# Early mod columns, sums behind splits, projection weights a step ahead, and grouped matmuls in a diffusion backbone

## The chip, the cores and the metric

The kernel runs on one core of a Trainium2 chip, with its engines TensorE (PE), VectorE (DVE), ScalarE (ACT), GpSimd (POOL) and SyncE (SP, which here issues all transfers). The metric is the device time of one execution in microseconds, as the median over runs. Lower is better.

## The reference, cut to what matters

Two layers over 256 latent tokens of width 2048, with 256 context tokens in the first layer. Layer 0 mixes by latent attention (8 heads, low-rank queries, keys and values) and by a multi-scale pooling, layer 1 by a Fourier transform; each layer ends with a squared-ReLU MLP of width 8192. Shifts, scales and gates come from a modulation of the condition `c`.

```
mod = silu(c) @ w_mod[l] + b_mod[l]              # 6 vectors of 2048 per layer
sh1, sc1, g1, sh2, sc2, g2 = split(mod, 6)
hx = rmsnorm(x, norm1[l]) * (1 + sc1) + sh1
# layer 0: px = hx @ w_in, pc = hc @ w_in (hc from the context, in the same way)
#   q  = rmsnorm(px[:512]) @ w_uq        kv = rmsnorm(p[512:768]) @ w_ukv
#   attention over 512 keys, 8 heads; pool = (window means - u) @ w_pool, u = px[832:]
#   y  = concat(attention, pool) @ w_out
# layer 1: y = real(fft2(hx in 4 channel groups)) @ w_out
x = x + g1 * y
x = x + g2 * square(relu((rmsnorm(x, norm2[l]) * (1 + sc2) + sh2) @ w1[l])) @ w2[l]
```

## The kernel before

Everything is held transposed, features on the 128 partitions and tokens along the columns. Weights arrive in float32, by 1 MB tiles into a ring of six buffers W (`load`, line 121). A tile is used as a sum of two rounded parts: `split` (line 131) has ScalarE cast a piece to H (line 135) and VectorE subtract, L = W − H (line 136), into two rings of six buffers. Activations are split likewise and hold both parts side by side, 256 columns each. One product of a weight block with the tokens is then, in `wide` (line 147), a 512-column matmul of H with both parts and a 256-column matmul of L with the high part, one after the other for each of two 128-row blocks k and each of four output banks j. `narrow` does the same in three 256-column matmuls.

The modulation vectors of which `mod_vector` makes a list are computed off TensorE: `mod_step` (line 93) loads 128 columns of `w_mod` into a W buffer, and `mod_sums` (line 99) has VectorE multiply it with the broadcast `cb` = silu(c) and sum it, one instruction of 2048 elements per column ("sum" below, line 103). `load` makes all sums outstanding before each weight transfer, and issues further columns at a rate `pace`.

The order of SP and TensorE is that of the program; the order of VectorE and ScalarE is set by a scheduler at build time, and each engine then works through its list in order.

The work goes in stages, by the trace: 0 to 152 us the modulation of layer 0 and the latents (`latents`, banks ka for keys, qa for queries, pu for the pooling's inputs), 152 to 399 attention woven with pooling and output projection (`weave`), 413 to 1104 the MLP of layer 0, 1104 to 1254 the Fourier layer and its output projection w_oo, 1266 to 1988 the MLP of layer 1.

The generator `attention` first computes squares, the variances (var), their reciprocal roots, spread over partitions (rb, copied to rk and rq), the normalised key latents kvf with their parts kvh and kvl, the query latents ql with parts qls, and the rotary key kr. `project(pr)` then loads the up-projections w_ukv and w_uq of two heads and multiplies: kn (keys), qr and qn (queries), v (values). `scores` (sc), `turned` (transposes tr) and `values` (pv) follow for each head. The generator `pooling` supplies the matmuls in between: four tiles w_pl[1, kt] (banks pu, line 467), each in two halves, then the window means with four tables `band`, w_pool, and the output projection w_oe.

Of the kernel before, what the change touches and what calls it, by code (L numbers as in the profile page):

```python
# [16 lines left out]
P = 128  # L17
T = 256
D = 2048
NB = D // P  # L20
# [23 lines left out]
def hybrid_dit(ctx: ExitStack, tc: tile.TileContext, xT, ctxT, c2, cb_in, vecs, wmod_s, wmod0, wmod1,  # L44
# [32 lines left out]
    def half(b, i):  # L77
        return b[:, i * T:(i + 1) * T]

    def mm(o, l, r, start, stop):  # L80
        nc.tensor.matmul(o, l, r, start=start, stop=stop, skip_group_check=True)  # L81


    todo, late = [], []
    pace = [0.0, 0.0]
    whole = set()

    def mod_vector(l, which, norm=None):
        src = wmod0[which - 2] if l == 0 else wmod1[which]
        for j in range(NB):  # L90
            todo.append((l, which, norm, j, src[j]))

    def mod_step():
        l, which, norm, j, src = todo.pop(0)
        w = wp.tile([P, 2048], F32, name="W", tag="W")
        nc.sync.dma_start(w, src)
        late.append((w, l, which, norm, j))

    def mod_sums():

        while late:
            w, l, which, norm, j = late.pop(0)
            nc.vector.scalar_tensor_tensor(w, w, 1.0, cb, ALU.mult, ALU.mult,  # L103
                                           accum_out=mods[l][:, which, j:j + 1])
            if j == NB - 1:
                whole.add((l, which))
                v = mods[l][:, which]
                b = V_BM[l] + which * NB
                nc.vector.tensor_tensor(v, v, vec[:, b:b + NB], ALU.add)
                if norm is not None:  # L110
                    scales(mods[l], which, norm)
# [7 lines left out]


    def load(src, n=2048):
        mod_sums()
        w = wp.tile([P, 2048], F32, name="W", tag="W")
        nc.sync.dma_start(w[:, :n], src)
        pace[1] += pace[0]
        while pace[1] >= 1 and todo:
            pace[1] -= 1
            mod_step()
        return w

    def split(w, lo, n, nn):

        h = hp.tile([P, 1024], F32R, name="H", tag="H")
        l = hp.tile([P, 1024], F32R, name="L", tag="L")
        nc.scalar.copy(h[:, :n], w[:, lo:lo + n])  # L135
        nc.vector.tensor_tensor(l[:, :n], w[:, lo:lo + n], h.bitcast(F32)[:, :n], ALU.subtract)  # L136
        return [(h[:, i:i + nn], l[:, i:i + nn]) for i in range(0, n, nn)]

    def split_act(u, src, n=T):
# [3 lines left out]
    def split_pair(h, l, src):  # L143
        nc.scalar.copy(h, src)
        nc.vector.tensor_tensor(l, src, h.bitcast(F32), ALU.subtract)

    def wide(ps, wts, j, acts, first, last):

        js = slice(j * P, (j + 1) * P)
        n = len(wts)  # L150
        for k, (h, l) in enumerate(wts):
            mm(ps, h[:, js], acts[k], first and k == 0, False)
            mm(ps[:, T:], l[:, js], acts[k][:, :T], False, last and k == n - 1)

    def narrow(o, wts, j, acts, first, last):

# [14 lines left out]
    def linear(tiles, acts, evac, nb=4, slim=False, drain=False):  # L171


        if slim:
            banks = [bank() for _ in range(nb // 2)]
            ps = [half(banks[j // 2], j % 2) for j in range(nb)]
        else:
            ps = [bank() for _ in range(nb)]
        for i, (srcs, k0) in enumerate(tiles):
            for s, src in enumerate(srcs):  # L180
                w = load(src)
                final = i == len(tiles) - 1
                for k in (0, 2):
                    wts = split(w, k * 512, 1024, 512)
                    first, last = i == 0 and k == 0, final and k == 2
                    part = acts[k0 + k:k0 + k + 2]
                    if drain and final:
                        if k == 0:
                            held = wts
                            yield  # L190
                            continue
                        wts, part = held + wts, acts[k0:k0 + 4]
                    for j in range(4):
                        o = ps[4 * s + j]
                        if slim:
                            narrow(o, wts, j, part, first and j % 2 == 0, last and j % 2 == 1)
                        else:
                            wide(o, wts, j, part, first, last)

                        if last and not slim:  # L200
                            evac(4 * s + j, o)
                        elif last and j % 2:
                            evac(4 * s + j - 1, ps[4 * s + j - 1])
                            evac(4 * s + j, o)
                    yield

    def run(steps):
        for _ in steps:
            pass
# [213 lines left out]
        lat = latents(g, wkq, wpl)  # L423
    nc.sync.dma_start(cb, cb_in)
    nc.scalar.activation(cb, cb, AF.Silu)
    run(lat)

    ropet = funit("ropet")
    nc.sync.dma_start(ropet.rearrange("p (a b) -> p a b", b=T), rope)
    bandt = [funit(f"band{i}") for i in range(4)]  # L430
    for i in range(4):
        nc.sync.dma_start(bandt[i], band[:, i])

    mod_vector(0, 2)
    mod_vector(0, 4, V_N2[0])
    mod_vector(0, 3)
    pace[0] = 1.75


# [27 lines left out]
    def pooling():  # L467

        ut = [[funit("ut") for hf in range(2)] for tb in range(2)]
        for tb in range(2):  # L470
            nc.scalar.copy(ut[tb][0], pu0[tb])
        us = [bank(f"pu{tb}") for tb in range(2)]
        for kt in range(4):
            w = load(w_pl[1, kt])
            for i in range(2):
                for n, (h, l) in enumerate(split(w, 1024 * i, 1024, 512)):
                    by_token(us, 4 * kt + 2 * i + n, h, l)
                yield
        for tb in range(2):
            nc.scalar.copy(ut[tb][1], us[tb])  # L480
        yield
        pooled = []
        for g in range(4):
            ps = bank("pl")
            for j in range(2):
                fs = slice((g % 2) * T + j * P, (g % 2) * T + (j + 1) * P)
                for tb in range(2):
                    mm(half(ps, j), ut[tb][g // 2][:, fs], half(bandt[g], tb), j == 0 and tb == 0, j == 1 and tb == 1)
            pooled.append(funit("pl"))
            nc.scalar.copy(pooled[g], ps)  # L490
            if g % 2:
                yield
        w = load(w_pool)
        for g in range(4):
            ps = bank("po")
            for j in range(2):
                plain(half(ps, j), [w[:, k * 256:(k + 1) * 256] for k in (2 * g, 2 * g + 1)], j,
                      [half(pooled[g], 0), half(pooled[g], 1)], j == 0, j == 1)
            for j in range(2):
                u = unit("mx")  # L500
                sc, o = column(V_PS + 2 * g + j), half(ps, j)
                nc.scalar.mul(u[:, :T], o, sc)
                nc.vector.scalar_tensor_tensor(u[:, T:], o, sc, u.bitcast(F32)[:, :T], ALU.mult, ALU.subtract)
                mixed.append(u)
            if g % 2:
                yield
        for ng in range(4):
            yield from linear([((w_oe[ng, kt],), 4 * kt - 8) for kt in (2, 3)], mixed,
                              residual(0, 2, None, True)(ng), 4, True)
# [4 lines left out]
    def rotary(s):  # L514
# [4 lines left out]
        nc.vector.tensor_tensor(r, r, half(ropet, 1), ALU.mult)  # L519
        nc.vector.tensor_tensor(s, s, r, ALU.add)  # L520

    def attention():
        squares = []
        for b in ka[:2] + qa:
            squares.append(funit("lq"))
# [26 lines left out]
            split_act(ql[j], f)  # L552
        kr = funit("kr")
        nc.scalar.copy(kr, ka[2])
        rotary(half(kr, 1))
        krh, krl = unit("krh"), unit("krl")
        split_pair(krh, krl, kr)
        yield 2

        def project(pr):  # L560

            w = load(w_ukv[pr], 1024)
            wkv = split(w, 0, 1024, 512)
            kn, vt = [], []
            for j in range(2):
                js = slice(j * P, (j + 1) * P)
# [5 lines left out]
                    mm(ps, l[:, js], kvh[k], False, k == 1)  # L572
                kn.append((unit("knh"), unit("knl")))
                split_pair(*kn[j], ps)
            w = load(w_uq[pr], 1536)
            wuq = split(w, 0, 768, 384) + split(w, 768, 768, 384)
            ps = bank("qr")
            narrow(half(ps, 0), wuq, 2, ql, True, True)
            f = scr("qr")
# [67 lines left out]
            split_act(a, o)  # L647
            attn.append(a)

        pair = project(0)  # L650
        yield 1
        p = scores((pair, 0))
        yield 2
        for h in range(NH):
            us = turned(p)
            head = (pair, h % 2)
            if h < NH - 1:
                if h % 2:
                    pair = project(h // 2 + 1)
                    yield 1  # L660
                p = scores((pair, (h + 1) % 2))
            else:
                yield 1
            values(head, us)
            yield 2
# [257 lines left out]
```

## Time and profile before

| what | value |
|---|---|
| median of 3 runs | 2003.67 us (2002.9 to 2005.29) |
| profiled execution | 2004.05 us |
| its span | 2002.3 us |
| TensorE busy | 1937.5 us, 97% |
| VectorE busy | 1461.3 us, 73% |
| ScalarE busy | 1025.0 us, 51% |
| read from memory | 533.69 MB, 268 GB/s over the span |

The busy time of an engine counts instructions that overlap only once. Matmuls are pipelined: each begins before the one ahead of it has ended, so the time that one costs is the distance between starts, not its duration.

### The profile page before, as it was taken

The numbers are of one execution on the slowest core, as the hardware profiler recorded it, in microseconds if no ns is written. First come the engines' busy times: TensorE is split into PE (matmuls) and PEld (weight loads), VectorE is DVE, ScalarE is ACT, GpSimd is POOL, SyncE is SP. The second block draws the span as 40 slices with busy tenths as digits, with TensorE's granted clock in tenths as the row PEclk, the third lists the DMA queues.
The fourth block names the chain that finished last, engine by engine and source line by source line (L and its number), as shares of the span: only waits on it lengthen the run. The fifth ranks groups of instructions, "written<-read, shape, count | busy, mean of one in ns | idle before, by whom it ended". The sixth has DMA issues, their size and how long they took to land.

```text
span 2002.3 us, 29622 instructions
## 1 busy us (share of the span) xinstructions
PE 1937.5 (97%) x11848; PEld 1702.7 (85%) x11848; DVE 1461.3 (73%) x2042; ACT 1025.0 (51%) x1655; POOL 1.2 (0%) x13
## 2 busy tenths in 40 slices
PE   5997999989999999999999999999999999999997
PEld 3886889978888888888888989788888888888887
DVE  4447999999888888888888577897555555555564
ACT  4334554455545645554555454555455446545653
POOL 0000000000000000000000000000000000000000
PEclk8998999989999999999999999899999999999998
DMA  9996899969889889888988247597555555555541
GB/s 377 370 385 235 324 365 336 340 237 388 320 336 344 338 311 345 323 326 315 335 326 316 85 171 271 186 386 289 178 193 184 184 186 189 190 189 182 182 163 43
DMA packets 77466, 537.71 MB, mean 269 GB/s; under 512 B 8848, under 2 KB 9104, under 8 KB 14480
## 3 DMA queue, kind: packets, MB, share of 16 engines
q1 hardware_dynamic: 77328, 535.82, 72.0%
q8 instruction: 92, 1.51, 0.3%
q14 instruction: 46, 0.38, 0.1%
HBM read 533.69 MB, written 2.10 MB: 268 GB/s over the span
## 4 chain that ended last, share of the span: by engine, by line
PE 92%; DVE 6%; DMA 1%; issue 1%; ACT 1%; SPq 0%; DVEq 0%; ACTq 0%
PE mm L81 80%; PE ka L81 2%; DVE W L103 2%; PE pu L81 2%; PE mrow L81 1%; DVE L L136 1%; PE qa L81 1%; PE f L81 1%; PE sc L81 1%; PE pv L81 1%; DMA W<-in_wmod_s 0%; PE var L81 0%; PE p L81 0%; PE pl L81 0%; DMA x<-in_xT 0%
## 5 line engine op out<-in xcount | busy, mean ns | idle before, releaser
L136 DVE TENSOR_TENSOR L<-W,H 128x1024 fp32r<-128x1024 f32 (+1 forms) x620 | 744.1, 1214 | 353.6 <-ACT H L135 353.0
L135 ACT CAST H<-W 128x1024 fp32r<-128x1024 f32 (+1 forms) x620 | 640.5, 1044 | 547.0 <-PE mm L81 498.1
L81 PE MATMUL mm<-h,H 128*128 128x512 f32 x2048 | 722.3, 397 | 3.6 <-DVE h L266 3.6
L81 PE MATMUL mm<-hid,H 128*128 128x512 f32 (+1 forms) x2176 | 718.4, 382 | 0.0
L81 PE MATMUL mm<-h,L 128*128 128x256 f32 x2048 | 576.6, 282 | 0.0
L81 PE MATMUL mm<-hid,L 128*128 128x256 f32 x2048 | 574.6, 281 | 0.0
L81 PEld LDWEIGHTS mm<-hid,H 128*128 128x128 f32 x2176 | 399.8, 188 | 84.5
L81 PEld LDWEIGHTS mm<-h,H 128*128 128x128 f32 x2048 | 386.5, 189 | 95.0 <-issue 2.1
L81 PEld LDWEIGHTS mm<-h,L 128*128 128x128 f32 x2048 | 389.5, 190 | 0.0
L81 PEld LDWEIGHTS mm<-hid,L 128*128 128x128 f32 x2048 | 387.4, 189 | 0.0
L103 DVE SCALAR_TENSOR_TENSOR W<-W,cb 128x2048 f32<-128x2048 f32 x160 | 364.7, 2282 | 0.0
L454 DVE SCALAR_TENSOR_TENSOR x<-mm,mods,x 128x256 f32<-128x256 f32 x176 | 80.2, 478 | 47.3 <-ACT rt L453 24.1
L453 ACT ACTIVATE rt<-mm,mods 128x256 f32<-128x256 f32 x132 | 61.8, 469 | 57.8 <-PE mm L81 56.1
L81 PE MATMUL mm<-fr,H 128*128 128x512 f32 (+1 forms) x320 | 91.0, 352 | 0.0
L692 ACT ACTIVATE rl<-g 128x256 f32<-128x256 f32 x128 | 53.2, 415 | 60.7 <-DVE g L690 59.4
L81 PE MATMUL mm<-fr,L 128*128 128x256 f32 x256 | 72.3, 282 | 1.5 <-DVE L L136 1.5
L689 ACT COPY b<-mm 128x256 f32<-128x256 f32 x128 | 45.6, 357 | 52.6 <-PE mm L81 52.6
L81 PEld LDWEIGHTS mm<-fr,H 128*128 128x128 f32 x320 | 55.8, 188 | 8.9
L690 DVE TENSOR_TENSOR g<-mm,b 128x256 f32<-128x256 f32 x128 | 53.4, 417 | 13.7 <-ACT b L689 13.6
L693 ACT ACTIVATE hd<-rl 128x256 f32<-128x256 f32 x128 | 53.2, 415 | 2.2
L141 DVE TENSOR_TENSOR hid<-hd,hid 128x256 fp32r<-128x256 f32 x128 | 53.5, 418 | 0.4
L140 ACT CAST hid<-hd 128x256 fp32r<-128x256 f32 x128 | 52.1, 407 | 1.0
(219 smaller groups left out, 1570.8 us busy)
## 6 DMA issues: line engine op xcount, KB each, us to landing
W<-in_w SPq DMA_DIRECT2D x256, 1024.0 KB, 5.0
W<-in_wmod SPq DMA_DIRECT2D x160, 1024.0 KB, 6.5
W<-in_wmod_s SPq DMA_DIRECT2D x32, 1024.0 KB, 9.6
W<-in_w_oe SPq DMA_DIRECT2D x16, 1024.0 KB, 7.3
W<-in_w_oo SPq DMA_DIRECT2D x16, 1024.0 KB, 4.9
W<-in_w_pl SPq DMA_DIRECT2D x8, 1024.0 KB, 7.0
W<-in_w_kq SPq DMA_DIRECT2D x8, 896.0 KB, 5.9
W<-in_w_uq SPq DMA_DIRECT2D x4, 768.0 KB, 4.5
```

The lines of the kernel that those rows point to most:

```text
L81: nc.tensor.matmul(o, l, r, start=start, stop=stop, skip_group_check=True)
L103: nc.vector.scalar_tensor_tensor(w, w, 1.0, cb, ALU.mult, ALU.mult, accum_out=mods[l][:, which, j:j + 1])
L135: nc.scalar.copy(h[:, :n], w[:, lo:lo + n])
L136: nc.vector.tensor_tensor(l[:, :n], w[:, lo:lo + n], h.bitcast(F32)[:, :n], ALU.subtract)
L140: nc.scalar.copy(u[:, :n], src)
L141: nc.vector.tensor_tensor(u[:, n:2 * n], src, u.bitcast(F32)[:, :n], ALU.subtract)
L453: nc.scalar.mul(t, half(ps, 1), g)
L454: nc.vector.scalar_tensor_tensor(x[:, i], ps[:, :T], g, x[:, i], ALU.mult, ALU.add)
L689: nc.scalar.copy(b, half(ps, 1))
L690: nc.vector.tensor_tensor(s, half(ps, 0), b, ALU.add)
L692: nc.scalar.activation(r, s, AF.Relu)
L693: nc.scalar.square(f, r)
```

## The change

- `cb` is now followed at once by the transfers of two modulation columns, ahead of the last step of the latents, and their sums are made right after it.
- `load` now makes only sums of columns that are at least two loads old; each `split` makes one sum of a column at least one load old, behind its own L.
- The four band tables, loaded in one block before, are loaded one at a time, after each tile of the pooling.
- The up-projections of a pair of heads are loaded and split by `pair_weights`: for pair 0 at the start of `attention`, for the others at the start of every odd head, ahead of its transposes. The rotation of kr comes after the first `project`.
- `linear` calls `wides` where it called `wide`: for a half-step of two k and four j, all eight H matmuls, and then all eight L matmuls. The evacuations follow in the second half.

VectorE, where the pooling starts. W with cb is a sum, h the last activation of the latents, va the first instruction after the variances. Before:

```order
L266 SCALAR_TENSOR_TENSOR h<-xr,mods_102,h 128x256
L136 TENSOR_TENSOR L<-W,H 128x1024 x2
L103 SCALAR_TENSOR_TENSOR W,mods_102<-W,cb 128x2048
L237 TENSOR_SCALAR va<-var 128x4
L237 TENSOR_SCALAR va<-var 128x2
```

After:

```order
L105 SCALAR_TENSOR_TENSOR W,mods_102<-W,cb 128x2048
L288 SCALAR_TENSOR_TENSOR h<-xr,mods_102,h 128x256
L105 SCALAR_TENSOR_TENSOR W,mods_102<-W,cb 128x2048
L139 TENSOR_TENSOR L<-W,H 128x1024
L105 SCALAR_TENSOR_TENSOR W,mods_102<-W,cb 128x2048
L139 TENSOR_TENSOR L<-W,H 128x768 x2
L105 SCALAR_TENSOR_TENSOR W,mods_102<-W,cb 128x2048 x2
L139 TENSOR_TENSOR L<-W,H 128x1024 x2
L105 SCALAR_TENSOR_TENSOR W,mods_102<-W,cb 128x2048
L259 TENSOR_SCALAR va<-var 128x4
```

The two L of 1024 columns before are those of the first pooling tile; after, they are the last such row, behind five sums and the L of w_ukv (1024) and w_uq (768 twice).

VectorE a little later, from the normalised latents to the second pooling tile. Before:

```order
L136 TENSOR_TENSOR L<-W,H 128x1024
L543 SCALAR_TENSOR_TENSOR kvf<-ka_113,vec,rk 128x512
L136 TENSOR_TENSOR L<-W,H 128x1024
L145 TENSOR_TENSOR kvl<-kvf,kvh 128x512
L543 SCALAR_TENSOR_TENSOR kvf<-ka_114,vec,rk 128x512
L549 SCALAR_TENSOR_TENSOR ql<-qa_111,vec,rq 128x256 x2
L145 TENSOR_TENSOR kvl<-kvf,kvh 128x512
L549 SCALAR_TENSOR_TENSOR ql<-qa_112,vec,rq 128x256 x2
L141 TENSOR_TENSOR qls<-ql,qls 128x256 x4
```

After:

```order
L574 SCALAR_TENSOR_TENSOR kvf<-ka_113,vec,rk 128x512
L580 SCALAR_TENSOR_TENSOR ql<-qa_111,vec,rq 128x256 x2
L150 TENSOR_TENSOR kvl<-kvf,kvh 128x512
L574 SCALAR_TENSOR_TENSOR kvf<-ka_114,vec,rk 128x512
L580 SCALAR_TENSOR_TENSOR ql<-qa_112,vec,rq 128x256 x2
L150 TENSOR_TENSOR kvl<-kvf,kvh 128x512
L146 TENSOR_TENSOR qls<-ql,qls 128x256 x4
L139 TENSOR_TENSOR L<-W,H 128x1024 x2
L105 SCALAR_TENSOR_TENSOR W,mods_102<-W,cb 128x2048 x2
L150 TENSOR_TENSOR knl<-kn,knh 128x512 x2
```

The two L of the second pooling tile stood ahead of and between the kvf, and now stand behind the last qls.

SP at the first pooling loads. Before:

```order
L429 DMA ropet<-in_rope 128x512
L432 DMA band_1499<-in_band 128x512
L432 DMA band_1500<-in_band 128x512
L432 DMA band_1501<-in_band 128x512
L432 DMA band_1502<-in_band 128x512
L124 DMA W<-in_w_pl 128x2048
L96 DMA W<-in_wmod 128x2048
L124 DMA W<-in_w_pl 128x2048
L96 DMA W<-in_wmod 128x2048 x2
L124 DMA W<-in_w_ukv 128x1024
```

After:

```order
L97 DMA W<-in_wmod 128x2048 x2
L457 DMA ropet<-in_rope 128x512
L127 DMA W<-in_w_ukv 128x1024
L97 DMA W<-in_wmod 128x2048
L127 DMA W<-in_w_uq 128x1536
L97 DMA W<-in_wmod 128x2048 x2
L127 DMA W<-in_w_pl 128x2048
L97 DMA W<-in_wmod 128x2048 x2
L502 DMA band_1505<-in_band 128x512
L127 DMA W<-in_w_pl 128x2048
L97 DMA W<-in_wmod 128x2048 x2
L502 DMA band_1506<-in_band 128x512
```

The first pooling tile comes behind five columns and the two up-projections, and from the second on a band stands ahead of each tile.

The diff, without the comments and the places that only follow from it:

```diff
+    loads = [0]
     def mod_step():
-        late.append((w, l, which, norm, j))
+        late.append((loads[0], w, l, which, norm, j))
-    def mod_sums():
-        while late:
-            w, l, which, norm, j = late.pop(0)
+    def mod_sums(n=NB, old=0):
+        while late and n and late[0][0] <= loads[0] - old:
+            n -= 1
+            _, w, l, which, norm, j = late.pop(0)
...
     def load(src, n=2048):
-        mod_sums()
+        mod_sums(NB, 2)
+        loads[0] += 1
...
     def split(w, lo, n, nn):
         nc.scalar.copy(h[:, :n], w[:, lo:lo + n])
         nc.vector.tensor_tensor(l[:, :n], w[:, lo:lo + n], h.bitcast(F32)[:, :n], ALU.subtract)
+        mod_sums(1, 1)
...
+    def wides(outs, wts, acts, first, last, done):
+        n = len(wts)
+        for j, ps in enumerate(outs):
+            for k, (h, _) in enumerate(wts):
+                mm(ps, h[:, j * P:(j + 1) * P], acts[k], first and k == 0, False)
+        for j, ps in enumerate(outs):
+            for k, (_, l) in enumerate(wts):
+                mm(ps[:, T:], l[:, j * P:(j + 1) * P], acts[k][:, :T], False, last and k == n - 1)
+            if last:
+                done(j)
...
     nc.scalar.activation(cb, cb, AF.Silu)
+    mod_vector(0, 2)
+    mod_vector(0, 4, V_N2[0])
+    mod_vector(0, 3)
+    for _ in range(2):
+        mod_step()
     run(lat)
+    mod_sums()
...
-    for i in range(4):
-        nc.sync.dma_start(bandt[i], band[:, i])
...
                 yield
+            nc.sync.dma_start(bandt[kt], band[:, kt])
...
+    def pair_weights(pr):
+        w = load(w_ukv[pr], 1024)
+        wkv = split(w, 0, 1024, 512)
+        w = load(w_uq[pr], 1536)
+        return wkv, split(w, 0, 768, 384) + split(w, 768, 768, 384)
     def attention():
+        ready = [pair_weights(0)]
...
-        pair = project(0)
+        pair = project()
+        rotary(half(kr, 1))
+        split_pair(krh, krl, kr)
...
         for h in range(NH):
+            if h % 2 and h < NH - 1:
+                ready.append(pair_weights(h // 2 + 1))
             us = turned(p)
```

## Rows read from the trace of the kernel before

**Rows 1.** The page: TensorE's busy time, share of the span, instructions.

```profile
PE 1937.5 (97%) x11848; PEld 1702.7 (85%) x11848; DVE 1461.3 (73%) x2042; ACT 1025.0 (51%) x1655; POOL 1.2 (0%) x13
```

**Rows 2.** Waits of TensorE: engine, line waited for, total us, times, longest us.

```profile
PE kn L81 <- DVE L L136: 7.0, 1, 7.0
...
PE mm L81 <- DVE L L136: 3.3, 3, 1.9
PE sc L81 <- DVE qnl L145: 3.1, 3, 1.7
...
PE qr L81 <- DVE L L136: 2.0, 1, 2.0
```

**Rows 3.** Windows: us; busy PE, PEld, DVE, ACT, POOL; PEclk, DMA share, GB/s.

```profile
143.00:176.00 33.00, 29.68 (x163) 25.72 (x162) 15.76 (x35) 15.89 (x26) 0.00 (x0) 0.90 0.55 216
150.00:200.00 50.00, 37.70 (x185) 32.12 (x184) 38.23 (x65) 21.00 (x33) 0.00 (x0) 0.83 0.61 235
300.00:400.00 100.00, 97.09 (x750) 94.39 (x749) 94.13 (x133) 44.85 (x69) 0.00 (x0) 0.98 0.91 338
1500.00:1550.00 50.00, 50.00 (x285) 43.36 (x285) 27.87 (x35) 29.33 (x53) 0.00 (x0) 1.00 0.53 187
```

**Rows 4.** Timeline of TensorE, MLP of layer 0 and 1: start, us, instruction.

```profile
599.89 0.39 PE L81 MATMUL mm<-h,H 128*128 128x512 f32 x1
...
605.78 0.39 PE L81 MATMUL mm<-h,H 128*128 128x512 f32 x1
...
1599.81 0.40 PE L81 MATMUL mm<-hid,H 128*128 128x512 f32 x1
...
1605.82 0.40 PE L81 MATMUL mm<-hid,H 128*128 128x512 f32 x1
```

**Rows 5.** Timeline of TensorE: values of pair 0 and what follows; Fourier layer.

```profile
196.32 0.28 PE L81 MATMUL v<-H,kvh 128*128 128x256 f32 x1
...
199.20 0.40 PE L81 MATMUL pu<-H,h 128*128 128x512 f32 x1
...
1144.95 0.40 PE L81 MATMUL f<-ch,h 128*128 128x512 f32 x1
...
1146.79 0.62 PE L81 MATMUL f<-ch,h 128*128 128x512 f32 x2
```

**Rows 6.** Timeline of TensorE, first pooling matmul with L; idle before, releaser.

```profile
155.54 0.50 PE L81 MATMUL pu<-L,h 128*128 128x512 f32 x1 [0.77 <-DVE L L136]
```

**Rows 7.** Timeline of ScalarE: cb's Silu, and the copy to rk.

```profile
143.07 1.92 ACT L425 ACTIVATE cb<-cb 128x2048 f32<-128x2048 f32 x1
...
169.19 0.58 ACT L538 COPY rk<-rb 128x512 f32<-128x512 f32 x1 [3.78 <-PE rb L81]
```

**Rows 8.** Groups by line and form, 150 to 240: busy us, mean ns.

```profile
L103 DVE SCALAR_TENSOR_TENSOR W<-W,cb 128x2048 f32<-128x2048 f32 x17 | 38.7, 2279 | 0.0
...
L136 DVE TENSOR_TENSOR L<-W,H 128x1024 fp32r<-128x1024 f32 x11 | 13.3, 1214 | 8.6 <-ACT H L135 8.6
L135 ACT CAST H<-W 128x1024 fp32r<-128x1024 f32 x12 | 12.3, 1045 | 3.9 <-DMA W<-in_w_pl 3.7 <-DMA W<-in_w_ukv 0.3
...
L136 DVE TENSOR_TENSOR L<-W,H 128x768 fp32r<-128x768 f32 x4 | 3.7, 943 | 0.0
```

**Rows 9.** Timeline of TensorE, projection of pair 0.

```profile
183.42 0.80 PE L81 MATMUL kn<-kvh,L 128*128 128x512 f32 x1 [6.96 <-DVE L L136]
...
184.44 0.63 PE L81 MATMUL kn<-kvl,H 128*128 128x512 f32 x1
184.86 0.63 PE L81 MATMUL kn<-kvh,L 128*128 128x512 f32 x1
...
190.51 0.39 PE L81 MATMUL qr<-qls,L 128*128 128x256 f32 x1 [2.03 <-DVE L L136]
```

**Rows 10.** Timeline of TensorE, projection of pair 1.

```profile
221.92 0.48 PE L81 MATMUL kn<-kvh,H 128*128 128x512 f32 x1
...
224.74 0.40 PE L81 MATMUL qr<-qls,H 128*128 128x256 f32 x2
```

More of the change, by code (lines that the diff above doesn't have):

```diff
@@ L192, in linear @@
                         wts, part = held + wts, acts[k0:k0 + 4]
+                    elif not slim:
+                        wides(ps[4 * s:4 * s + 4], wts, part, first, last,
+                              lambda j: evac(4 * s + j, ps[4 * s + j]))
+                        yield
+                        continue
                     for j in range(4):
@@ L430, in hybrid_dit @@
     bandt = [funit(f"band{i}") for i in range(4)]
-    for i in range(4):
-        nc.sync.dma_start(bandt[i], band[:, i])
-    mod_vector(0, 2)
-    mod_vector(0, 4, V_N2[0])
-    mod_vector(0, 3)
     pace[0] = 1.75
@@ L554, in attention, with project @@
         nc.scalar.copy(kr, ka[2])
-        rotary(half(kr, 1))
         krh, krl = unit("krh"), unit("krl")
-        split_pair(krh, krl, kr)
         yield 2
-        def project(pr):
-            w = load(w_ukv[pr], 1024)
-            wkv = split(w, 0, 1024, 512)
+        def project():
+            wkv, wuq = ready.pop()
             kn, vt = [], []
@@ L574, in project @@
                 split_pair(*kn[j], ps)
-            w = load(w_uq[pr], 1536)
-            wuq = split(w, 0, 768, 384) + split(w, 768, 768, 384)
             ps = bank("qr")
@@ L658, in attention @@
                 if h % 2:
-                    pair = project(h // 2 + 1)
+                    pair = project()
                     yield 1
```

## The prediction

> **What bounds the kernel now.** I read first the page's busy shares: TensorE is busy 1937.5 us, 97% of the span, and VectorE 73% [rows 1]. So the time is TensorE's matmuls at their spacing, plus its pauses, plus what it does at the lower of its two clock levels (1.2 instead of 2.4 GHz). The waits of TensorE by releaser come next [rows 2]: after the start the large ones are kn on the L of a split, 7.0 us, and qr on L, 2.0; the mm matmuls wait 3.3 on L, the scores 3.1 on qnl. Third are the stretches by window [rows 3]: in 150–200 TensorE is busy for 37.7 of 50 us at a granted clock of 0.83; in 300–400 it is busy for 97 of 100, at 0.98. So the change touches two separate things: the spacing of the matmul pairs in the MLPs, and the stretch from 143 to 240, where attention's first projections and the pooling start.
>
> **Grouped matmuls.** A pair is one 512-column matmul with H and one 256-column matmul with L. Durations in the trace overlap, so I take start to start. In layer 0, 17 pairs go from 599.89 to 605.78, or 346.5 ns each; in layer 1 from 1599.81 to 1605.82, or 353.5 [rows 4]. Grouped, eight 512s are followed by eight 256s. The Fourier layer shows 512s that follow a 256: eight starts from 1144.95 to 1146.79, 1.84 us [rows 5]. For 256s after each other, the 24 of v take from 196.32 to 199.20, 0.12 us each [rows 5]; eight take 0.96, and as the first after a 512 comes a little earlier I take 0.95. A group is 2.79 us, 349 ns per pair. There are 1984 such pairs in each MLP and 192 in w_oo, which I put at layer 1's spacing: 1984 × 2.5 ns = +5.0 us, 1984 × −4.5 = −8.9, 192 × −4.5 = −0.9: **−4.8 us**. This is a small difference of large numbers. If both layers came to 346.5 in the grouped order it would be about −15, at 353.5 in both about +14. I keep both ends; 349 lies between them and is made of measured starts.
>
> The Trainium skill ("TensorE: Matmul & The Clock Gate", section "Back-to-back issue gap") gives N/2.4 + 2.5 ns for an isolated gap at the high clock, by which a pair would take about 325 ns (an estimate) in either order and grouping would be worth nothing. The rows show 346.5 and 353.5 for one and the same pair, so the formula leaves something out here.
>
> L is also needed 8 × 0.23 = 1.84 us after H and no longer 0.23 after it. This hides about half of the 3.3 us for which mm waits on L [rows 2]: **−1.5 us** (bounds 0 and −3.3). The evacuations of four banks now come closer together; VectorE is busy 27.9 and ScalarE 29.3 of 50 us in layer 1 [rows 3], so I count them at nothing. Without that cover TensorE would wait at most once per output group of 32 in an MLP.
>
> **Two columns and pair 0 ahead of the pooling weights.** Before, TensorE's first second-half pooling matmul with an L starts at 155.54 [rows 6]. After, VectorE works in this order: sum, h, sum, L of w_ukv, sum, two L of w_uq, two sums, and only then that L. The first sum can't start before cb's Silu, which runs from 143.07 for 1.92 us [rows 7]. With 2.28 us for a sum, 1.21 and 0.94 for an L of 1024 and of 768 columns [rows 8] and about 0.4 for h: 5 × 2.28 + 0.4 + 1.21 + 2 × 0.94 + 1.21 = 16.1, so 161.1, and TensorE has its L at about 161.2: **+5.7 us**. The load can't be sooner either: its W buffer is that of the second column. VectorE was busy for only 15.8 of the 33 us from 143 to 176 [rows 3]; the sums fill idle time of VectorE, but ahead of the one thing that TensorE waits for there.
>
> From the variances to rk (169.19 [rows 7]) the same chain follows, 5.7 later, at about 174.9. Then comes what the change buys. Before, TensorE had the next pooling step until 176.5, then waited 6.96 us for w_ukv's L, which VectorE made behind two sums, and later 2.03 for w_uq's [rows 9]. Both splits are now long done. But the L of w_pl[1,1] now stand on VectorE behind two kvf, two kvl, four ql, four qls, some 6 us, plus their own 1.21 [rows 8]: TensorE has the rest of its pooling step only from about 182. Then 24 matmuls × 0.23 = 5.5 us, kn 12 × 0.23, qr and qn 36 × 0.12, v 2.88 [rows 5]: 197.5 at full speed. Before, v ended at 199.2 [rows 5], although kn behind the long pause ran at half speed (0.42 us from 184.44 to 184.86 [rows 9]). With a slow stretch of that kind behind the new pause too, some 4 us dearer, it ends at 201.4. I take this, as the pause is about as long: **+2.2 us** against before at this point, the 5.7 included; the bounds are −1.7 and +2.2.
>
> **Behind v.** H of w_pl[1,2] now stands on ScalarE behind the second v copy and krh (each about 0.55, as rk's copy [rows 7]), then takes 1.05, then L takes 1.21 [rows 8], of which one matmul covers 0.23: **+3.3**. The next pooling load is held on SP's queue by a band, which stands in front of it and waits for a buffer: **+0.6**. In pair 1's projection kn at 221.92 and qr at 224.74 had waited for nothing [rows 10]. After, H of w_ukv stands on ScalarE behind the two copies of the transposes (1.1), takes 1.05, then L, partly covered: **+2.6**. On VectorE L of w_uq stands behind a sum, two knl (about 0.65 each), another sum and needs 0.94: 6.8, less the 2.4 that kn's rest covers: **+4.4**. Of the scores' 3.1 us on qnl [rows 2] about two thirds should go, as qn is ready earlier against the sums: **−2.0**. Together **+11.1 us** for the stage. Bounds: −4, where the four waits after v stay out, and +16, where each is followed by slow matmuls.
>
> **Sum.** −4.8 − 1.5 + 11.1 = +4.8 on the profiled execution's 2004.05 us gives 2008.9; the median of the runs is 0.4 lower: **2008.5 us**.
>
> **Rivals.** *VectorE's idle time comes back.* The place is kn's wait at 176–183. What TensorE waited for there were sums on VectorE, and 17.2 us of idle time [rows 3] ahead of them now hold such sums. The price: 6.96 + 2.03, and about 3.7 for the matmuls that ran slowly behind these two waits, against +5.7: −7.0, and with the matmuls −13.3: 1990. It decides if w_pl[1,1] is split before TensorE is through with w_pl[1,0], and the later splits equally. For it: both long waits go for certain. Against: the order on ScalarE and VectorE, which puts these splits behind the chain.
> *The loss is made up later.* TensorE idles 2.9 us in 300–400 [rows 3], which a late start can absorb, and v may end at 197.5: 11.1 − 2.9 − 3.9 = +4.3, so 2001.7. Against it: VectorE is busy for 94 of 100 us there and can't run ahead.
> *Grouping is worth nothing*, as by the page's rule: 2013.3; at 353.5 in both layers 2027.
> *Slow matmuls follow each new wait.* For it: they followed both waits in [rows 9]. Three more at 1.7: 2013.6.
>
> **Chances.** Forecast 0.46 (own range 2004 to 2013), idle time comes back 0.18, made up later 0.20, grouping worth nothing or less 0.10, slow matmuls 0.06. About 0.2%, 4.0 us, is what a measurement here can tell from no change, so "same" is 1999.7 to 2007.7. Faster: 0.18, and 0.04 of the made-up case, 0.22. Same: the rest of that case, 0.16, and 0.12 of the forecast: 0.28. Slower: 0.50. The range from 1995 to 2017 leaves out about half of the first rival and the case of 353.5.
>
> **What would show it.** Right: TensorE's first pooling matmul with L near 161 and a pause of some 6 us in front of the second pooling step's; no wait of kn on L near 176, but waits in pair 1's kn on H and qr on L; pairs at 349 ns in both layers, so that layer 0's MLP starts 11 us late and ends 16 late, and layer 1 gives 9 back. Wrong: v ending before 196, a projection of pair 1 without waits, or a grouped pair outside 347 to 351 ns.

## The result and the profile after

The changed kernel takes 2020.38 us (2019.79 to 2022.27, 4 runs) against 2004.34 for the kernel before: a ratio of 1.0082, 95% interval 1.0065 to 1.0100. It is slower, as forecast, but by 16 us instead of 5 and outside the range. The profiled execution of the changed kernel took 2022.27 us, that of before 2004.05; the 18 us between these two are what the traces below explain.

First the page's busy shares, which answer to [rows 1]: TensorE is busy about as long as before, so little of the loss is matmul work as such.

```profile
PE 1941.3 (96%) x11848; PEld 1714.9 (85%) x11848; DVE 1460.7 (72%) x2042; ACT 1016.7 (50%) x1655; POOL 1.2 (0%) x13
```

The starts of the stages' first matmuls, read from TensorE's timeline, show where the time goes (up to the latents the profiled execution of the changed kernel is 0.4 us shorter, so the first step is that much larger):

| first matmul of | before, us | after, us | later by | change in the step | forecast for the step |
|---|---|---|---|---|---|
| pooling behind pair 0 (end of v) | 199.20 | 204.37 at v's end, 206.67 with the wait behind it | 5.2 at v's end | +5.2 | +2.2 |
| qn of pair 1 | 226.17 | 245.91 | 19.7 | +14.6 | +10.9 |
| output projection with at | 349.39 | 368.29 | 18.9 | −0.8 | −2.0 |
| MLP of layer 0 | 407.80 | 432.26 | 24.5 | +5.6 | 0 |
| w_oo | 1157.61 | 1186.35 | 28.7 | +4.3 | +5.0 |
| MLP of layer 1 | 1261.65 | 1287.70 | 26.1 | −2.7 | −2.4 |
| final norm | 1988.20 | 2006.18 | 18.0 | −8.1 | −8.9 |

The matmul part came out as worked out, −6.5 against −6.3. The stage up to the MLP of layer 0 lost 24.5 us instead of 11.1. TensorE's waits in that stage (143 to 432.4; line waited for, us in total, times, longest), which answer to [rows 2]:

```profile
PE pu L81 <- ACT H L138: 14.6, 4, 5.9
PE mm L81 <- DVE L L139: 6.3, 4, 2.8
PE pu L81 <- DVE L L139: 4.7, 4, 2.8
PE qr L81 <- DVE L L139: 2.6, 1, 2.6
...
PE kn L81 <- ACT H L138: 1.7, 1, 1.7
...
PE sc L81 <- DVE qnl L150: 1.3, 1, 1.3
```

kn's wait of 7 us on L is gone, as is more than half of sc's. Pooling matmuls wait four times on H and four times on L, where they had waited once for each (1.6 and 0.8 us); new are waits in pair 1's projection, and longer ones of mm on L at the output projection. All rows of this view add up to 38.8 us, those of before in the same stage to 24.3: 14.5 of the 24.5 us are pauses. What is left, 10, fits with more matmuls at the lower clock, of which the windows tell; they answer to [rows 3]:

```profile
143.00:176.00 33.00, 24.70 (x117) 21.60 (x117) 24.15 (x37) 11.52 (x16) 0.00 (x0) 0.71 0.76 306
150.00:200.00 50.00, 34.62 (x142) 28.66 (x141) 33.17 (x56) 14.92 (x26) 0.00 (x0) 0.73 0.49 194
300.00:400.00 100.00, 96.90 (x727) 93.63 (x726) 92.91 (x134) 46.36 (x77) 0.00 (x0) 0.98 0.91 337
```

The granted clock from 143 to 176 fell from 0.90 to 0.71 and from 150 to 200 from 0.83 to 0.73. VectorE, which did 24.2 us of work instead of 15.8 from 143 to 176, did 33.2 instead of 38.2 from 150 to 200: work was moved ahead, but then it ran short of work.

Grouped pairs in TensorE's timeline (start, us), which answer to [rows 4]:

```profile
601.98 2.00 PE L81 MATMUL mm<-hid,H 128*128 128x512 f32 x8
...
604.77 1.55 PE L81 MATMUL mm<-hid,H 128*128 128x512 f32 x6
...
1600.45 2.00 PE L81 MATMUL mm<-hid,H 128*128 128x512 f32 x8
1602.29 1.12 PE L81 MATMUL mm<-hid,L 128*128 128x256 f32 x8
1603.24 2.00 PE L81 MATMUL mm<-hid,H 128*128 128x512 f32 x8
```

A group of eight 512s and eight 256s takes 2.79 us in both layers (601.98 to 604.77, 1600.45 to 1603.24): 349 ns per pair, of which the 512s take 1.84 and the 256s 0.95 (1602.29).

The stage's matmuls that the forecast spoke of, which answer to [rows 5, 6, 9, 10]:

```profile
161.08 0.79 PE L81 MATMUL pu<-L,h 128*128 128x512 f32 x1 [2.76 <-DVE L L139]
...
162.53 0.63 PE L81 MATMUL pu<-L,h 128*128 128x512 f32 x1
162.95 1.05 PE L81 MATMUL pu<-H,h 128*128 128x512 f32 x2
...
186.22 0.80 PE L81 MATMUL pu<-H,h 128*128 128x512 f32 x1 [5.93 <-ACT H L138]
...
206.67 0.49 PE L81 MATMUL pu<-H,h 128*128 128x512 f32 x1 [2.14 <-ACT H L138]
...
245.91 0.63 PE L81 MATMUL qn<-qls,H 128*128 128x256 f32 x2
```

The first pooling matmul with L starts at 161.08, against a forecast of 161.2. It is followed by matmuls 0.42 us apart (162.53 to 162.95), nearly twice the usual 0.23. At the second tile TensorE waits for H until 186.22.

What the forecast had not weighed stands in SP's queue. Its waits from 150 to 230 (line 502 issues a band):

```profile
SPq L502 <- PE pu L81: 41.1, 2, 31.6
SPq L502 <- DVE krl L150: 13.2, 1, 13.2
```

And its timeline (start, us, transfer):

```profile
155.50 0.33 SPq L127 DMA_DIRECT2D W<-in_w_pl  x1
157.70 2.54 SPq L97 DMA_DIRECT2D W<-in_wmod  x2
191.91 0.33 SPq L502 DMA_DIRECT2D band<-in_band  x1
192.33 0.38 SPq L127 DMA_DIRECT2D W<-in_w_pl  x1
...
206.43 0.33 SPq L502 DMA_DIRECT2D band<-in_band  x1
206.81 0.43 SPq L127 DMA_DIRECT2D W<-in_w_pl  x1
```

A band waits until a buffer of its pool is released, here by a pooling matmul or by krl, for 31.6 us in one case. For all that time nothing behind it is issued: between 160 and 191.9 SP issues no transfer at all, between 193 and 206.4 none either. The third pooling tile goes out at 192.33, right behind its band, and the fourth at 206.81.

These pauses of TensorE aren't waits for data under way, though. The second tile, issued at 155.50, has landed after 9.4 us, at 164.9, and the third after 5.8, at 198.1; ScalarE casts them only at 185.13 and 205.57. Its timeline at the third:

```profile
205.05 0.62 ACT L149 CAST krh<-kr 128x512 fp32r<-128x512 f32 x1
205.57 1.99 ACT L138 CAST H<-W 128x1024 fp32r<-128x1024 f32 x2
```

ScalarE works through its list, in which these casts stand behind the copies of v and krh. The fourth tile (landed at 212.0, cast at 217.92) and pair 1's w_ukv (222.9, 232.61) are alike. So the bands must act at least in part through the order of the lists, to which the experiment on the queue returns.

### The profile page after: what moved, and what is told of

Its sections match the earlier page's. It is cut to its first block, busy times and chain, and to the rows that moved or that the text cites. A ratio compares the mean times of both kernels' runs of the same rounds, so it can differ in the third digit from the quotient of the medians.

```text
span 2020.2 us, 29636 instructions
## 1 busy us (share of the span) xinstructions
PE 1941.3 (96%) x11848; PEld 1714.9 (85%) x11848; DVE 1460.7 (72%) x2042; ACT 1016.7 (50%) x1655; POOL 1.2 (0%) x13
## 4 chain that ended last, share of the span: by engine, by line
PE 94%; DVE 3%; ACT 1%; DMA 1%; issue 1%; SPq 0%; DVEq 0%; ACTq 0%
PE mm L81 79%; PE pu L81 2%; PE ka L81 2%; PE mrow L81 1%; PE f L81 1%; PE sc L81 1%; PE qa L81 1%; DVE L L139 1%; DVE W L105 1%; PE pv L81 1%; PE kn L81 1%; PE p L81 1%; PE var L81 1%; PE qn L81 0%; DMA W<-in_wmod_s 0%
## 5 line engine op out<-in xcount | busy, mean ns | idle before, releaser
L81 PE MATMUL mm<-hid,H 128*128 128x512 f32 (+1 forms) x2176 | 526.9, 379 | 0.0
L81 PE MATMUL mm<-h,H 128*128 128x512 f32 x2048 | 516.6, 394 | 3.6 <-DVE h L288 3.6
L81 PEld LDWEIGHTS mm<-hid,H 128*128 128x128 f32 x2176 | 385.3, 189 | 61.7
L81 PEld LDWEIGHTS mm<-h,H 128*128 128x128 f32 x2048 | 370.7, 190 | 70.7 <-issue 2.1
L81 PE MATMUL mm<-hid,L 128*128 128x256 f32 x2048 | 303.9, 282 | 0.0
L81 PEld LDWEIGHTS mm<-hid,L 128*128 128x128 f32 x2048 | 286.5, 190 | 18.7
L81 PEld LDWEIGHTS mm<-h,L 128*128 128x128 f32 x2048 | 280.8, 191 | 20.2
L81 PE MATMUL mm<-h,L 128*128 128x256 f32 x2048 | 286.7, 283 | 0.0
L81 PE MATMUL mm<-fr,H 128*128 128x512 f32 (+1 forms) x320 | 71.2, 349 | 0.0
L81 PE MATMUL pu<-H,h 128*128 128x512 f32 x128 | 50.7, 451 | 14.6 <-ACT H L138 14.6
```

## Experiments

The theories: (1) pair 0's splits and the sums ahead of the pooling's first split on VectorE starve TensorE, as forecast, and slow matmuls raise the price; (2) the bands in SP's queue hold up the pooling tiles and all columns behind them; (3) the sums behind every split make the next one late. Kernels with grouped matmuls are compared with each other. Their own times agree within some 2 to 7 us, while those of alternating kernels fall into groups (last section).

**Grouping alone.** The kernel before with `wides`:

```diff
+                    elif not slim:
+                        wides(ps[4 * s:4 * s + 4], wts, part, first, last,
+                              lambda j: evac(4 * s + j, ps[4 * s + j]))
...
```

> The kernel before, with the grouped matmuls alone. If a grouped pair takes 349 ns in both layers and L is needed 1.84 us later at w_oo's start, the MLP of layer 0 takes 4 to 5 us longer, w_oo some 2 less, layer 1 some 8 less: about 1998 us, 6 below before. If grouping is worth nothing by itself and the whole loss of the changed kernel had been larger elsewhere, about 2003. The stage from 143 to 408 must read as before, with kn's wait of 7 us.

Measured: 1997.69 us (1996.61 to 1998.37, 12 runs), ratio to before 0.9965 (0.9938 to 0.9992). kn waits 7.0 us as before. The grouping is what it was worked out to be, −6.3 against an execution of 2004; the changed kernel's other parts cost 22.7 us.

**No grouping.** The changed kernel with `wide`:

```diff
-                    elif not slim:
-                        wides(ps[4 * s:4 * s + 4], wts, part, first, last,
...
```

> The changed kernel with H and L alternating as before. Additive: 2020.4 + 6.3 = about 2026.5, with pairs at 346.5 ns in layer 0 and 353.5 in layer 1. If the two parts of the change work on each other (grouping delaying the prefetch or the evacuations), less than 2024 or more than 2030.

Measured: 2038.64 us, but the six runs are 2012.89, 2026.20, 2038.09, 2039.20, 2041.68 and 2041.70. 2026.2 is the sum that was expected, and the others lie about 14 us to either side. By the expectation, more than 2030 would mean that the two parts work on each other; the three groups of the last section would explain the spread without that. The profiled execution is the fastest. Its pairs (TensorE's timeline, one of layer 0 and one of layer 1):

```profile
599.79 0.39 PE L81 MATMUL mm<-hid,H 128*128 128x512 f32 x1
...
605.68 0.39 PE L81 MATMUL mm<-hid,H 128*128 128x512 f32 x1
...
1599.89 0.39 PE L81 MATMUL mm<-hid,H 128*128 128x512 f32 x1
...
1605.78 0.39 PE L81 MATMUL mm<-hid,H 128*128 128x512 f32 x1
```

Seventeen pairs take 5.89 us in both layers. In the kernel before that was so in layer 0 alone [rows 4]. So 346.5 and 353.5 don't belong to the layers, as the prediction had it, but to the execution.

**Up-projections inside the projection again.** The calls of `pair_weights` and the moved rotation are taken out of the changed kernel:

```diff
-        ready = [pair_weights(0)]
...
-            wkv, wuq = ready.pop()
+            w = load(w_ukv[pr], 1024)
+            wkv = split(w, 0, 1024, 512)
...
```

> The changed kernel with the up-projections loaded and split inside the projection again, the rotation of kr ahead of it, and all else as changed (early columns, sums behind splits, bands between the pooling tiles, grouping). Theory 1, that pair 0's splits and the sums behind them stand ahead of the pooling's first split on VectorE and that slow matmuls follow each pause: the first pooling L comes before 156, and most of the 25 us goes, 1998 to 2006. Theory 2, that the bands in SP's queue hold the pooling tiles: the pauses at the second to fourth pooling tile stay, 2010 to 2016. Theory 3, that sums behind every split delay the next one: also 2010 or more, with VectorE's sums named ahead of the pauses.

Measured: 2017.63 us (2016.54 to 2020.29, 12 runs). Only 2.8 us of the loss go, and theory 1 falls; the time lies 1.6 us above theory 2's range too. The first pooling matmuls now come early, but TensorE waits 8.7 us for H of the second tile. SP's timeline:

```profile
134.51 0.33 SPq L97 DMA_DIRECT2D W<-in_wmod  x1
156.20 0.33 SPq L502 DMA_DIRECT2D band<-in_band  x1
156.62 0.38 SPq L127 DMA_DIRECT2D W<-in_w_pl  x1
```

And ScalarE's at that tile:

```profile
175.43 0.62 ACT L149 CAST krh<-kr 128x512 fp32r<-128x512 f32 x1 [2.07 <-DVE kr L544]
175.95 2.94 ACT L138 CAST H<-W 128x1024 fp32r<-128x1024 f32 x3
```

Behind the column at 134.51 the first band waits for TensorE's first pooling half-step, and the second tile goes out at 156.62. In the kernel before, by SP's timeline, it went out 20 us earlier:

```profile
136.60 0.33 SPq L124 DMA_DIRECT2D W<-in_w_pl  x1
```

The late tile has landed after 6.6 us, at 163.2. The rest of the delay is ScalarE's list, which has its cast behind krh.

**The old rule for sums** in the changed kernel:

```diff
-        mod_sums(NB, 2)
+        mod_sums()
...
-        mod_sums(1, 1)
```

> The changed kernel with the old rule for sums: every load makes all outstanding sums, no split makes any. Theory 1: pair 0's weights still come first, and the sums stand ahead of loads instead; the pauses at 157 to 186 stay, 2014 to 2022. Theory 3: the stage falls back by more than half of the loss, 2008 or less. Theory 2: unchanged, 2018 to 2022.

Measured: 2015.66 us (2014.51 to 2018.77, 12 runs), 4.7 less than changed. The new rule costs something here, but theory 3, which asked for 2008 or less, doesn't carry the loss. Theory 2 had expected no change.

**Bands in front.** The changed kernel, with the bands in one block behind the rope table:

```diff
     bandt = [funit(f"band{i}") for i in range(4)]
+    for i in range(4):
+        nc.sync.dma_start(bandt[i], band[:, i])
...
-            nc.sync.dma_start(bandt[kt], band[:, kt])
```

> The changed kernel with the four bands loaded in one block right behind the rope table again, all else as changed. Theory 2 (each band waits in SP's queue for a free buffer that TensorE's pooling step gives, and the next pooling tile, the columns and the up-projections wait behind it): the pauses of 5.9, 2.9 and 2.0 us at the second to fourth pooling tile and those at pair 1's projection go, 2000 to 2008; the first pooling L stays near 161. Theory 1 (pair 0's splits ahead of the pooling's first split are the main cost): 2012 to 2020.

Measured: 1989.59 us (1987.54 to 1992.30, 10 runs), ratio to before 0.9950 (0.9925 to 0.9976). This is 30.8 us less than the changed kernel and 8.1 less than the grouping alone. It went further than theory 2 expected. The first tile still comes late on TensorE:

```profile
159.92 0.80 PE L81 MATMUL pu<-H,h 128*128 128x512 f32 x1 [7.93 <-ACT H L138]
164.39 0.79 PE L81 MATMUL pu<-L,h 128*128 128x512 f32 x1 [3.67 <-DVE L L139]
```

These are waits of 7.9 and 3.7 us, so the first matmul with L is even later than after the change (164.39 against 161.08). But it is the last such pause: the waits at the other pooling tiles, at pair 1's projection and at the output projection are gone but for 0.4 us on one L. SP issues the third and fourth tile in time:

```profile
165.50 0.33 SPq L127 DMA_DIRECT2D W<-in_w_pl  x1
...
173.88 0.33 SPq L127 DMA_DIRECT2D W<-in_w_pl  x1
```

**Bands in front, no early pairs.** Two edits together:

```diff
+    for i in range(4):
+        nc.sync.dma_start(bandt[i], band[:, i])
...
-        ready = [pair_weights(0)]
...
```

> Bands in front, and the up-projections inside the projection: what is left of the change is the two early columns, the sums behind the splits, and the grouping. If bands and pair 0 are the whole loss: 1994 to 1999 (the grouped kernel alone gave 1997.7), with kn waiting for w_ukv's L again but shorter. Theory 3 (sums behind splits): 2003 or more, with the waits at the output projection's L still 6 us.

Measured: 1992.52 us (1991.77 to 1993.74, 10 runs). This is less than either expectation. Early columns and the sums behind splits are together worth 5.2 us against the grouping alone; theory 3 fails here too.

**Early pairs alone.** The changed kernel with bands in front, the old rule for sums, and no early columns:

```diff
+        nc.sync.dma_start(bandt[i], band[:, i])
...
-        mod_sums(NB, 2)
+        mod_sums()
...
-    for _ in range(2):
-        mod_step()
     run(lat)
-    mod_sums()
```

> Grouping and the up-projections ahead, without the other parts (bands in front, old rule for sums, no early columns). Theory 1: the first pooling L comes behind w_ukv, w_uq and three sums, near 158 to 161, and 2002 to 2010 results. If the placement is good once SP is free: the waits of kn and qr (9 us and slow matmuls) go for less than they cost, 1988 to 1996.

Measured: 1994.15 us (1992.83 to 1996.93, 10 runs): 3.5 less than the grouping alone. The up-projections ahead, pair 0's and the later pairs' together, are a gain once SP is free.

**Bands in front, old rule for sums:**

```diff
+        nc.sync.dma_start(bandt[i], band[:, i])
...
-        mod_sums(NB, 2)
+        mod_sums()
...
```

> As the run with the bands in front, and the old rule for sums. In the changed kernel the old rule was worth 4.7 us. If sums behind splits cost by themselves (VectorE late at the end of the output projection), again 3 to 5 us less than with the bands in front alone; if they cost only as VectorE had been kept idle by SP, the same within 1.5 us.

Measured: 1991.77 us (1988.43 to 1995.42, 10 runs) against 1989.59 with the new rule. The medians differ by 2.2 us the other way, with ranges that overlap: the rule that cost 4.7 us with SP blocked shows no cost without.

**The queue or the transfer?** The changed kernel, with each band at its late place and still waiting for a buffer, but on GpSimd's queue:

```diff
-            nc.sync.dma_start(bandt[kt], band[:, kt])
+            nc.gpsimd.dma_start(bandt[kt], band[:, kt])
```

> The changed kernel with the bands at the same places of the program and waiting for the same buffers, but issued from GpSimd's queue instead of SP's. If it is the queue, in which the pooling tiles stand behind a waiting band, the time is that of the kernel with the bands in front, 1987 to 1993. If it is the band's late arrival, its buffer, or the traffic of the transfers, the time stays near the changed kernel's, 2015 to 2021.

Measured: 1987.40 us (1985.07 to 1989.09, 10 runs), 33 us less than the changed kernel by one word; ratio to before 0.9945 (0.9908 to 0.9982). GpSimd's timeline shows two bands waiting about as long as on SP (31.6 and 13.2 us there):

```profile
184.89 0.54 POOL L502 DMA_DIRECT2D band<-in_band  x1 [34.73 <-PE pu L81]
197.54 0.54 POOL L502 DMA_DIRECT2D band<-in_band  x1 [12.11 <-PE pu L81]
```

And SP's shows the third and fourth pooling tile going out regardless:

```profile
162.32 0.33 SPq L127 DMA_DIRECT2D W<-in_w_pl  x1
...
171.92 0.33 SPq L127 DMA_DIRECT2D W<-in_w_pl  x1
```

So it is the bands' place in SP's queue, and not their lateness, their buffers or their traffic. One step that the prediction priced separately turns out to hang on it as well. VectorE's timeline in this kernel:

```profile
175.36 2.35 DVE L139 TENSOR_TENSOR L<-W,H 128x1024 fp32r<-128x1024 f32 x2
179.72 0.75 DVE L574 SCALAR_TENSOR_TENSOR kvf<-ka,vec,rk 128x512 f32<-128x512 f32 x1 [2.00 <-ACT rk L569]
```

And in the changed kernel:

```profile
179.56 0.75 DVE L574 SCALAR_TENSOR_TENSOR kvf<-ka,vec,rk 128x512 f32<-128x512 f32 x1 [4.24 <-ACT rk L569]
...
184.17 1.43 DVE L146 TENSOR_TENSOR qls<-ql,qls 128x256 fp32r<-128x256 f32 x4
186.21 2.36 DVE L139 TENSOR_TENSOR L<-W,H 128x1024 fp32r<-128x1024 f32 x2 [0.61 <-ACT H L138]
```

With the bands off SP, the scheduler puts the L of the second tile ahead of kvf; with them on SP it put them behind qls. ScalarE's casts of that tile move likewise, from 185.13 to 173.64. So the order on which the 6 us pause at the second tile rested followed from the bands' place on SP. The one word changed two things, then: what SP holds back as the program runs, and the lists that were built. No run has late bands on SP with the other lists, so how the 33 us divide between the two is not shown.

**Late bands alone.** The grouped kernel before, and only the bands moved:

```diff
-    for i in range(4):
-        nc.sync.dma_start(bandt[i], band[:, i])
...
+            nc.sync.dma_start(bandt[kt], band[:, kt])
```

> The kernel before with the grouped matmuls and one further edit: the bands one by one behind the pooling tiles, on SP. If the late bands alone are enough for the loss: 2012 to 2025, against 1997.7 for the grouped kernel. If they only hurt together with pair 0's early weights or the sums behind the splits: 1997 to 2003.

Measured: 2017.55 us (2015.89 to 2020.83, 10 runs), +19.9 against the grouping alone. The late bands on SP are enough for nearly the whole loss of 22.7. SP's timeline:

```profile
131.42 0.43 SPq L96 DMA_DIRECT2D W<-in_wmod  x1
155.95 0.33 SPq L494 DMA_DIRECT2D band<-in_band  x1
156.33 0.42 SPq L124 DMA_DIRECT2D W<-in_w_pl  x1
```

**The first pooling tile ahead of pair 0**, with the bands in front. The edit puts pair 0's transfers behind the first tile's, but its splits behind that tile's first half only:

```diff
     def attention():
-        ready = [pair_weights(0)]
...
         yield 1
+        ready = [pair_weights(0)]
```

> The kernel with the bands in front, and pair 0's up-projections behind the pooling's first tile instead of ahead of it. The pauses of 7.9 and 3.7 us at the first pooling tile should go, with the slow matmuls behind them; if nothing takes their place 1976 to 1984. If the chain from the variances to rk and the splits in VectorE's list take their place: 1986 to 1993.

Measured: 1994.60 us (1993.36 to 1995.09, 10 runs), 5.0 more than with pair 0 first. This run missed both expectations. The long pauses of the first tile go, but new waits of pooling matmuls take their place (whole kernel):

```profile
PE pu L81 <- DVE L L139: 9.5, 3, 6.1
PE pu L81 <- ACT H L138: 5.9, 3, 2.9
```

One short wait of each kind is at the first tile's first half; the others come at its second half, whose split stands behind pair 0's, and at the second tile. Letting the pooling's start be late, and everything behind it early, was the better order.

## Why the prediction was wrong

- **Grouping.** Right: 349 ns in both layers, +4.3 and −8.1 where +5.0 and −8.9 were worked out. That the two sides can be compared layer by layer is partly luck: +5.0 and −8.9 hold against the one execution of before that was profiled, and others run their layers at other spacings (last section). The −1.5 for the later L came out as well (−2.7 at w_oo, with the −0.9), but as the whole 1.5 us that mm had waited there, not as half of all waits. The Trainium skill ("TensorE: Matmul & The Clock Gate", section "Back-to-back issue gap") gives N/2.4 + 2.5 ns for an isolated matmul at the high clock, about 325 ns for a pair in either order (an estimate). The traces don't agree: the same pairs take 346.5, 349 or 353.5 ns.
- **The start of the pooling.** Right in place and size, 161.08. Left out of the sum were the slow matmuls from 162 to 177; the prediction had them behind the second pause only. So the copy to rk came at 178.94 and not at 174.9, and v ended at 204.4 and not at 201.4.
- **"The next pooling load is held on SP's queue by a band … +0.6".** This is the step that failed. The second to fourth band wait for 31.6, 13.2 and 9.5 us, and while one waits, nothing behind it in the queue is issued. Taking the bands off SP gave 33.0 us, moving them to the front 30.8, and the late bands alone cost 19.9. The prediction saw the row in SP's order and priced it for one tile alone. It didn't ask how long a buffer stays taken, nor count the columns and up-projections that stand behind; and it took the lists of VectorE and ScalarE as they were, without asking what had made them. The stage's loss passed even the upper bound of +16: of the 13.4 us too little, 3.0 lie ahead of v's end, 3.7 up to qn of pair 1, 1.2 up to the output projection and 5.6 behind its start. With the bands on GpSimd's queue the MLP of layer 0 starts at 399.63 and not at 432.26, so all of it hangs on where the bands stand.
- **The pause at the second tile, and H behind v.** Forecast at about 6 and 3.3 us; found at 5.9 in front of the second tile, and behind v at 2.1 for H and 0.8 for L. The sizes were right, and TensorE did wait for VectorE's and ScalarE's order, as forecast. What the forecast didn't see is that this order came with the bands' place on SP.
- **Pair 1's projection.** Forecast 2.6 and 4.4, found 2.2 and 4.0, followed by slow matmuls: 14.6 in the step up to qn instead of 10.9.
- **Recovery.** Forecast −2.0 up to the MLP; found +4.8. VectorE was short of work until 240 (busy for 24.1 of 40 us from 200 to 240, 37.9 before), and late with the L of the output projection, which stood behind sums (mm on L, 6.3 instead of 1.9 in this stage).
- **The rival that idle time comes back** had −7.0 for the stage. With the bands loaded in front it is what happens: 1989.6 against 1997.7, −8.1. That the sizes agree is partly luck, as the first pooling matmul with L is then later than the rival had it (164.39). The rest of the change is good; one transfer's place turned it into a loss.

Of the loss of 24.5 us in the stage the waits account for 14.5. That the other 10 are the slow matmuls is by subtraction, and the granted clock agrees. Of the signs that were to show the prediction wrong none appeared, and of those that were to show it right only the MLP's start failed, at 24.5 us late and not 11: they tested the pauses that had been counted, not what made them.

## What to carry to other kernels

A transfer that waits for a buffer holds every transfer behind it on its queue, so its price goes by how long it waits and what stands behind it, not by its own bytes; look at when its buffer comes free, or issue it from an idle engine's queue. Where a scheduler orders the other engines, compare their lists too: moving one transfer changed them here. In this stage the added pauses cost more than their length, about two thirds more (10 us beside 14.5, by subtraction), in slow matmuls. If a change of several parts loses, first undo the part that was costed at next to nothing.

## What the runs showed of the hardware that was not expected

A 512-column matmul alternating with a 256-column one ran at one of two spacings wherever a layer was looked at, 346.5 or 353.5 ns per pair, and layer 1 differs in that between two profiled executions with the same order of matmuls. The 85 executions of the kernel before that were timed beside the experiments fall into three groups: 33 at 1988.7 to 1993.2, 40 at 2002.0 to 2005.7, 12 at 2015.9 to 2019.2. The steps between their averages are 13.4 and 13.5 us, and 1984 pairs × 7.0 ns = 13.9. One profiled execution has both layers at 346.5, another one layer at each; a third, with both at 353.5, wasn't profiled. So it is inferred, not shown, that the slow group is this one, and that the groups come from the spacing. What decides it stays open. In groups of eight the pairs take 349 ns in the profiled executions, and the ten or twelve runs of the grouped kernels spread over 2 to 7 us. The 85 executions average about 2001 us and the grouped kernel alone takes 1997.7, so grouping is worth some 3 us on average and takes away the spread; the comparison by which this change was measured happened to meet the middle group. Against the fast group, about 1990.7 on average, grouping alone is 7 us slower.
